# Inverse square roots of norms in a filter stage: Newton steps by column on VectorE, or Ln and Exp on ScalarE with one Newton step over all columns

## The chip, the cores and the metric

The kernel runs on one core of one Trainium2 chip. The metric is the device time of one execution in microseconds (us). The engines are named as in the profile: PE (TensorE), DVE (VectorE), ACT (ScalarE), POOL (GpSimd) and SP, each with an instruction queue of its own that is worked off in order.

## The reference

A hybrid encoder layer on x of shape (1, 1024, 1024) in float32: RMSNorm, one input projection, an S5 state-space branch, a Hyena branch with two long implicit filters, a gated merge, an output projection and a final RMSNorm. Two normalisations matter here. Each long filter is scaled by the inverse norm of its channel, and the rows of x by their inverse root mean square:

```python
def rmsnorm(x, w):
    xf = x.astype(jnp.float32)
    y = xf * lax.rsqrt(jnp.mean(xf * xf, axis=-1, keepdims=True) + RMS_EPS)
    return (y * w.astype(jnp.float32)).astype(x.dtype)

def hyena_filters(...):
    ...
    h = h * (jnp.exp(-t * jnp.abs(decay.astype(f32))) + HY_SHIFT)
    ...
    k = k * lax.rsqrt(jnp.sum(k * k, axis=0, keepdims=True) + HY_EPS)
    return jnp.fft.rfft(k, axis=0)
```

## The kernel before, in words

The kernel is one Python program that a scheduler turns into a queue of instructions for each engine. The scheduler orders by the place in the program and by readiness in its own model of time; `tc.high_priority(offset=40)` counts a block as if it were written 40 instructions earlier, and `tc.issue_after(ins)` keeps a block behind one given instruction on that engine. Buffers of a pool go round among tiles of one tag.

The first 245 us or so are the filter stage (`filters`). There are eight units, two filter orders by four quarters of 256 channels. For unit u, `filter_time` makes the filter in time in eight steps of 128 time rows: two matmuls into a PSUM tile `g` of two buffers (L333, L334), the decay by Exp on ACT (L336, tile `e`, three buffers), the product on DVE (L338), the squares on ACT (L342), sums and differences `so`, `ss`, `sd` on DVE or POOL (L349, L350), a split into a high part on ACT (L109, tile `sh`) and a low part on DVE (L113, tile `sl`), and the running sum of squares `acc` on POOL (L357, L362). `filter_freq` transforms the unit before: 48 matmuls for each of two halves of odd frequencies (L404), `even` matmuls (L414), and joins on DVE (L425 to L430). Work on the rows of x runs between the steps (`norm_in`): squares on ACT (L457), the inverse roots of eight columns (L463), scaling on ACT (L468), transposes on PE into PSUM tiles of tag `xt` (L475, two buffers), and splits (L479, L480).

`filters` steps through twelve positions i per unit, each with a piece of `filter_time` for unit u, of `filter_freq` for unit u - 1, and at every third position of `norm_in`. At i = 0 stands the norm of unit u - 1 (`filter_norm`): matmuls with a column of ones add `acc` over the partitions into tile `q` (L371, tag `xt` too), DVE adds 1e-6 (L375), `rsqrt` takes two columns (L377), and then a second part follows: two products on DVE (L381), two transposes on PE (L383) and a correction of one row of `ss` on DVE (L386), which the even matmuls with tile 0 read, at position 5. After the eighth unit both parts run with nothing of `filter_time` beside them, and the weights for the rest are then prefetched.

`rsqrt` starts from an integer estimate (L119), multiplies v by -0.5 (L121) and makes three Newton steps; each takes two instructions for every column (L125, L126), since the factor v stands as a scalar operand for each partition. A call with 2 columns has 2 + 3 x 2 x 2 = 14 instructions, the call of `norm_in` with 8 columns 50. There are eight of the one and one of the other. After the filter stage come the S5 blocks, the transforms and the projections, of which PE's queue is full.

Of the kernel before, what the change touches and what calls it, by code (L numbers as in the profile page):

```python
# [11 lines left out]
I32 = mybir.dt.int32  # L12
ALU = mybir.AluOpType
AF = mybir.ActivationFunctionType
# [86 lines left out]
class Trunk:  # L101
# [12 lines left out]

    def rsqrt(self, pool, out, v, n):

        V = self.nc.vector
        h = pool.tile([128, n], F, name="rsq_h", tag="rsq_h")
        V.tensor_scalar(out=out.bitcast(I32), in0=v.bitcast(I32), scalar1=-0.5, scalar2=float(0x5F3759DF),  # L119
                        op0=ALU.mult, op1=ALU.add)  # L120
        V.tensor_scalar(out=v, in0=v, scalar1=-0.5, scalar2=None, op0=ALU.mult)  # L121
        for _ in range(3):
            for c in range(n):
                y, z = out[:, c:c + 1], h[:, c:c + 1]
                V.scalar_tensor_tensor(out=z, in0=y, scalar=v[:, c:c + 1], in1=y, op0=ALU.mult, op1=ALU.mult)  # L125
                V.scalar_tensor_tensor(out=y, in0=z, scalar=1.5, in1=y, op0=ALU.add, op1=ALU.mult)  # L126

    def reduce_2pi(self, out, x, k):
        nc = self.nc
# [113 lines left out]
    def filters(self, ctx, top):  # L243
        tc = self.tc
# [9 lines left out]
        units = [(o, cq) for o in range(2) for cq in range(4)]  # L254
        sds = {}
        x = self.norm_in()
        for u in range(len(units) + 1):
# [16 lines left out]
            if u > 1:  # L274
                f, f0 = self.filter_freq(*units[u - 1], sds), 0
            if u == len(units):
                self.filter_norm(*units[u - 1], sds)
                c2.close()
                self.weight_pools(top)
                self.proj_pools(top)  # L280
                self.prefetch()
            for i in range(12):
                next(t, None)
                if i == 0 and u < len(units):
                    with tc.high_priority(offset=40):
                        self.filter_norm(*units[u - 1], sds)
                if i >= f0:
                    with tc.issue_after(self.f_g.ins):
                        next(f)
                if i % 3 == 0:  # L290
                    with tc.issue_after(self.f_sq.ins):
                        next(x, None)
                if i == 6 and u + 1 < len(units):
                    self.filter_load(*units[u + 1])()
# [70 lines left out]
    def filter_norm(self, o, cq, sds):  # L365
# [9 lines left out]
        nc.vector.tensor_scalar(out=qs, in0=q[:, 0:2], scalar1=1e-6, scalar2=None, op0=ALU.add)  # L375
        nrm = self.nrm[:, col:col + 2]
        self.rsqrt(up, nrm, qs, 2)  # L377
        r = q[:, NCH:]
        for ct in range(2):
            c = slice(ct, ct + 1)  # L380
# [1159 lines left out]
```

## Time and profile before

| | us |
|---|---|
| median of 3 runs | 1415.73 |
| lowest and highest | 1414.94, 1419.7 |
| the profiled execution | 1413.96 |
| its span in the trace | 1412.2 |
| busy in the span: PE, DVE, ACT, POOL | 1346.7, 1014.1, 515.1, 416.6 |
| granted TensorE clock, mean | 0.986 of full speed |

The profile is of one execution. A group row gives line, engine, operation, output and inputs with shapes and the count, then busy time in us and mean ns of one, then the idle time of the engine just before them and what ended it. In the windows, the two numbers after the stretch's name are its length and then the busy time of each engine with the number of its instructions.

### The profile page before, as it was taken

Reading aid. Unit: us, or ns where it says so; the run is one execution under the profiler, and the core shown is the slowest. Engines: PE = TensorE matmul, PEld = TensorE weight load, DVE = VectorE, ACT = ScalarE, POOL = GpSimd, SP = SyncE. Lnnn points to the kernel's source line nnn. Section 1 sums busy time; section 2 is a strip of 40 time slices with the busy share of each in tenths; the row PEclk is TensorE's granted clock in tenths of the full one; section 3 lists DMA queues with packets and bytes.
Section 4 is the critical chain, followed back from the end, with each engine's and each line's share of the span. In section 5 each row is a group of like instructions: output and inputs, shape, how many; then the busy total and the mean of one; then the engine's idle time right before and its main releaser. Section 6 shows DMA issues by size and latency. Waiting matters only on the chain.

```text
span 1412.2 us, 19536 instructions
## 1 busy us (share of the span) xinstructions
PE 1346.7 (95%) x7219; PEld 1135.9 (80%) x7219; DVE 1014.1 (72%) x1934; ACT 515.1 (36%) x737; POOL 416.6 (29%) x343
## 2 busy tenths in 40 slices
PE   5888899999999999999999997999999999999997
PEld 3777798888888887788788885998888889878886
DVE  7999997699599887414479997663899836843632
ACT  5576664222332333333322222443222234422422
POOL 3766675000000000223112213743013223322322
PEclk9999999999999999999999998999999999999999
DMA  8222224865695554566985588769888988755431
GB/s 278 94 78 75 77 100 146 200 173 137 164 301 132 124 124 103 134 173 155 307 244 173 172 241 264 216 179 315 258 268 268 292 247 245 220 161 134 139 112 64
DMA packets 188556, 257.24 MB, mean 182 GB/s; under 512 B 23069, under 2 KB 144153, under 8 KB 185724
## 3 DMA queue, kind: packets, MB, share of 16 engines
q1 hardware_dynamic: 148492, 151.32, 34.0%
q0 software_dynamic: 12608, 43.79, 15.6%
q10 hardware_dynamic: 27360, 60.88, 12.0%
q8 instruction: 57, 0.93, 0.3%
q14 instruction: 39, 0.32, 0.1%
HBM read 147.49 MB, written 76.82 MB: 159 GB/s over the span
## 4 chain that ended last, share of the span: by engine, by line
PE 72%; DVE 18%; DMA 5%; issue 3%; ACT 1%; POOL 1%; SPq 0%; ACTq 0%; DVEq 0%; POOLq 0%
PE pps L556 43%; PE ops L1441 6%; PE iv L643 5%; PE po L404 4%; PE fwo L695 3%; DMA zc<-c_zc_lo_d 2%; PE pe L414 2%; PE pps L536 2%; DVE rsq_h L125 2%; DVE e L338 1%; PE fwe L695 1%; DMA d_y<-x 1%; DVE st L1274 1%; PE zt L680 1%; DVE st L1272 1%
## 5 line engine op out<-in xcount | busy, mean ns | idle before, releaser
L512 POOL DMA_DIRECT2D wlo<-wraw x76 | 66.3, 872 | 673.3 <-ACT wlo L511 530.2
L556 PE MATMUL pps<-xh,whi 128*128 128x512 f32 x848 | 214.2, 400 | 3.2 <-DVE cv L581 3.2
L556 PE MATMUL pps<-xl,whi 128*128 128x512 f32 x848 | 212.3, 397 | 0.0
L556 PE MATMUL pps<-xh,wlo 128*128 128x512 f32 x848 | 210.2, 396 | 0.0
L556 PEld LDWEIGHTS pps<-xh,whi 128*128 128x128 f32 x848 | 158.0, 189 | 39.5 <-ACT wlo L511 3.6
L556 PEld LDWEIGHTS pps<-xh,wlo 128*128 128x128 f32 x848 | 157.9, 188 | 36.8
L556 PEld LDWEIGHTS pps<-xl,whi 128*128 128x128 f32 x848 | 157.3, 188 | 36.3 <-issue 0.2
L510 ACT CAST whi<-wraw 128x1024 fp32r<-128x1024 f32 (+1 forms) x76 | 74.7, 982 | 285.7 <-PE pps L556 254.9
L404 PE MATMUL po<-sh,fo 128*128 128x256 f32 x512 | 101.1, 292 | 6.0 <-DVE sh L111 5.1
L643 PE MATMUL iv<-ic,y 128*128 128x256 f32 (+1 forms) x752 | 97.2, 287 | 5.5 <-POOL y L113 3.1
L643 PEld LDWEIGHTS iv<-ic,y 128*128 128x128 f32 x752 | 95.4, 194 | 8.1 <-POOL y L113 4.0
L404 PEld LDWEIGHTS po<-sh,fo 128*128 128x128 f32 x512 | 84.0, 197 | 8.3 <-DVE sh L111 6.1
L357 POOL TENSOR_TENSOR acc<-acc,sq 128x512 f32<-128x512 f32 x56 | 75.9, 1356 | 24.5 <-ACT sq L342 23.0
L511 ACT ACTIVATE wlo<-whi 128x1024 fp32r<-128x1024 f32 (+1 forms) x76 | 74.9, 985 | 20.7 <-PE pps L556 20.6
L113 DVE TENSOR_TENSOR y<-yraw,y 128x512 fp32r<-128x512 f32 x60 | 55.0, 938 | 28.2 <-ACT y L109 28.2
L404 PE MATMUL po<-sl,fo 128*128 128x256 f32 x256 | 74.2, 290 | 1.0 <-DVE sl L113 1.0
L579 DVE SCALAR_TENSOR_TENSOR cv<-pps,cw,cv 128x1023 f32<-128x1023 f32 x24 | 30.7, 1281 | 59.5 <-ACT cv L578 59.5
L109 ACT CAST y<-yraw 128x512 fp32r<-128x512 f32 x64 | 39.0, 619 | 55.9 <-DMA yraw<-d_y 27.4
L404 PEld LDWEIGHTS po<-sl,fo 128*128 128x128 f32 x256 | 50.4, 197 | 2.2 <-DVE sl L113 1.3
L578 ACT ACTIVATE cv<-pps,cb,cw 128x1024 f32<-128x1024 f32 x24 | 29.0, 1208 | 62.1 <-PE pps L556 43.9
L333 PE MATMUL g<-w3h,ha 128*128 128x512 f32 x64 | 33.3, 520 | 18.6 <-DVE e L338 17.6
L695 PE MATMUL fwo<-z,zc 128*128 128x256 f32 x384 | 49.9, 283 | 0.0
(447 smaller groups left out, 2788.7 us busy)
## 6 DMA issues: line engine op xcount, KB each, us to landing
wlo<-wraw POOLq DMA_DIRECT2D x64, 512.0 KB, 5.7
wraw<-w_in SPq DMA_DIRECT2D x56, 512.0 KB, 5.2
kspec<-ko SPq DMA_DIRECT2D x32, 512.0 KB, 3.6
kt<-kspec SPq DMA_DIRECT2D x32, 512.0 KB, 5.1
yraw<-d_y SPq DMA_DIRECT2D x64, 256.0 KB, 5.3
d_y<-x ACTq DMA_DIRECT2D x28, 512.0 KB, 5.5
d_m<-cv ACTq DMA_DIRECT2D x16, 512.0 KB, 2.6
d_z<-z ACTq DMA_DIRECT2D x8, 1024.0 KB, 5.5
```

The costliest lines, as they stand in the source:

```text
L109: nc.scalar.copy(out=hi, in_=src)
L113: e.tensor_tensor(out=lo, in0=src, in1=hi, op=ALU.subtract)
L333: nc.tensor.matmul(out=ps, lhsT=ha[:, tsl], rhs=w3h, start=True, stop=False)
L357: nc.gpsimd.tensor_tensor(out=acc, in0=acc, in1=sq, op=ALU.add)
L404: nc.tensor.matmul(out=po[:, part], lhsT=fo[a][:, 12 * (jj % 2) + b], rhs=sd[4 + i][d][:, part], start=n == 0 and part == 0, stop=n == 11 ...
L510: nc.scalar.copy(out=hi, in_=raw)
L511: nc.scalar.activation(out=lo, in_=hi, func=AF.Copy, scale=-1.0)
L512: nc.gpsimd.dma_start(out=lo, in_=raw, accum_op=ALU.add)
L556: self.summed = nc.tensor.matmul(out=ps[:, hf * 512:hf * 512 + 512], lhsT=w[:, kc], rhs=part(x, kc, hf), start=a == 0 and p == 0 and kc == ...
L643: self.rotated = nc.tensor.matmul(out=dst, lhsT=lhsT, rhs=self.ic[b, j][:, cols], start=first, stop=last)
L695: nc.tensor.matmul(out=out, lhsT=zc[a][:, b], rhs=z[:, :, d, zi], start=start and n == 0, stop=stop and n == 3 * len(prods) - 1)
L1441: nc.tensor.matmul(out=pss[cs.start][:, 0:cs.stop - cs.start], lhsT=m[:, kc, ts], rhs=w[kc][:, cs], start=kc == 0 and p == 0, stop=kc == 7 ...
```

## The change

`rsqrt` takes the logarithm of all columns and then the exponential of -0.5 times it, both on ACT, in place of the integer estimate, and makes one Newton step of three DVE instructions over all columns in place of three steps by column. `filter_norm` becomes a generator with one stop, behind `rsqrt`; `filters` runs its first part at i = 0 as before and its second part at i = 3, with the same priority, ahead of that position's piece of `filter_freq`. After the last unit both parts run one after the other.

```diff
--- before.py
+++ after.py
@@ -114,16 +114,14 @@
 
     def rsqrt(self, pool, out, v, n):
 
-        V = self.nc.vector
+        nc, V = self.nc, self.nc.vector
         h = pool.tile([128, n], F, name="rsq_h", tag="rsq_h")
-        V.tensor_scalar(out=out.bitcast(I32), in0=v.bitcast(I32), scalar1=-0.5, scalar2=float(0x5F3759DF),
-                        op0=ALU.mult, op1=ALU.add)
+        nc.scalar.activation(out=h, in_=v, func=AF.Ln)
+        nc.scalar.activation(out=out, in_=h, func=AF.Exp, scale=-0.5)
         V.tensor_scalar(out=v, in0=v, scalar1=-0.5, scalar2=None, op0=ALU.mult)
-        for _ in range(3):
-            for c in range(n):
-                y, z = out[:, c:c + 1], h[:, c:c + 1]
-                V.scalar_tensor_tensor(out=z, in0=y, scalar=v[:, c:c + 1], in1=y, op0=ALU.mult, op1=ALU.mult)
-                V.scalar_tensor_tensor(out=y, in0=z, scalar=1.5, in1=y, op0=ALU.add, op1=ALU.mult)
+        V.tensor_tensor(out=h, in0=out, in1=out, op=ALU.mult)
+        V.tensor_tensor(out=h, in0=h, in1=v, op=ALU.mult)
+        V.scalar_tensor_tensor(out=out, in0=h, scalar=1.5, in1=out, op0=ALU.add, op1=ALU.mult)
 
     def reduce_2pi(self, out, x, k):
         nc = self.nc
@@ -274,7 +272,8 @@
             if u > 1:
                 f, f0 = self.filter_freq(*units[u - 1], sds), 0
             if u == len(units):
-                self.filter_norm(*units[u - 1], sds)
+                for _ in self.filter_norm(*units[u - 1], sds):
+                    pass
                 c2.close()
                 self.weight_pools(top)
                 self.proj_pools(top)
@@ -283,7 +282,11 @@
                 next(t, None)
                 if i == 0 and u < len(units):
                     with tc.high_priority(offset=40):
-                        self.filter_norm(*units[u - 1], sds)
+                        norm = self.filter_norm(*units[u - 1], sds)
+                        next(norm)
+                if i == 3 and u < len(units):
+                    with tc.high_priority(offset=40):
+                        next(norm, None)
                 if i >= f0:
                     with tc.issue_after(self.f_g.ins):
                         next(f)
@@ -375,6 +378,7 @@
         nc.vector.tensor_scalar(out=qs, in0=q[:, 0:2], scalar1=1e-6, scalar2=None, op0=ALU.add)
         nrm = self.nrm[:, col:col + 2]
         self.rsqrt(up, nrm, qs, 2)
+        yield
         r = q[:, NCH:]
         for ct in range(2):
             c = slice(ct, ct + 1)
```

## Rows read from the trace of the kernel before

**Rows 1.** The page: PE and DVE over the span, and in forty slices
```profile
PE 1346.7 (95%) x7219; PEld 1135.9 (80%) x7219; DVE 1014.1 (72%) x1934; ACT 515.1 (36%) x737; POOL 416.6 (29%) x343
...
PE   5888899999999999999999997999999999999997
...
DVE  7999997699599887414479997663899836843632
```

**Rows 2.** Busy time by engine, between the norms' starts; last row all seven
```profile
45.40:70.50 25.10, 21.47 (x119) 18.23 (x120) 24.65 (x50) 15.91 (x27) 19.30 (x19) 0.93 0.31 111
70.50:98.40 27.90, 24.40 (x149) 21.39 (x149) 26.22 (x50) 23.73 (x58) 18.90 (x20) 0.96 0.26 92
98.40:132.90 34.50, 28.81 (x168) 25.10 (x168) 33.73 (x103) 17.24 (x30) 19.79 (x21) 0.88 0.22 83
132.90:160.70 27.80, 25.77 (x160) 23.03 (x160) 27.25 (x52) 19.77 (x36) 18.48 (x20) 0.94 0.23 80
160.70:185.90 25.20, 22.20 (x144) 19.76 (x144) 24.06 (x51) 16.83 (x30) 20.78 (x20) 1.00 0.21 72
185.90:213.10 27.20, 27.14 (x184) 24.76 (x184) 27.10 (x55) 19.09 (x32) 20.45 (x23) 1.00 0.25 96
213.10:237.50 24.40, 23.01 (x152) 20.59 (x151) 22.87 (x47) 10.71 (x19) 17.50 (x18) 1.00 0.22 87
45.40:237.50 192.10, 172.80 (x1066) 152.87 (x1067) 185.87 (x398) 123.29 (x225) 135.20 (x139) 0.96 0.24 88
```

**Rows 3.** Who waited for whom, 45 to 245 us: total, times, longest
```profile
ACT sq L342 <- DVE e L338: 19.1, 12, 5.5
...
PE g L333 <- DVE e L338: 12.8, 9, 3.1
...
PEld pe L414 <- DVE ss L386: 2.5, 3, 1.1
```

**Rows 4.** The chain that ended last, 45 to 245 us, by line
```profile
by line: PE po L404 19.8%; PE pe L414 12.6%; DVE rsq_h L125 12.1%; DVE e L338 9.3%; issue 5.7%; DVE sl L113 5.0%; DVE nrm L126 3.7%; DVE ko L429 2.6%; DVE xl L480 2.6%; PE g L333 2.5%; DVE ko L430 2.4%; PE g L334 2.1%; DVE so L350 2.1%; DVE
```

**Rows 5.** Groups of DVE instructions by line, 0 to 260 us
```profile
L125 DVE SCALAR_TENSOR_TENSOR rsq_h<-nrm,qs 128x1 f32<-128x1 f32 x48 | 21.9, 490 | 0.2
...
L126 DVE SCALAR_TENSOR_TENSOR nrm<-rsq_h,nrm 128x1 f32<-128x1 f32 x48 | 10.2, 233 | 0.0
L125 DVE SCALAR_TENSOR_TENSOR rsq_h<-rs,ssq 128x1 f32<-128x1 f32 x24 | 8.2, 358 | 0.0
...
L126 DVE SCALAR_TENSOR_TENSOR rs<-rsq_h,rs 128x1 f32<-128x1 f32 x24 | 4.4, 196 | 0.0
...
L119 DVE TENSOR_SCALAR nrm<-qs 128x2 int32<-128x2 int32 x8 | 3.1, 384 | 0.1
```

**Rows 6.** Instructions in order of time, DVE then POOL, from 46 us
```profile
46.05 1.42 DVE L125 SCALAR_TENSOR_TENSOR rsq_h<-nrm,qs 128x1 f32<-128x1 f32 x2
47.39 0.27 DVE L126 SCALAR_TENSOR_TENSOR nrm<-rsq_h,nrm 128x1 f32<-128x1 f32 x2
...
46.18 2.62 POOL L357 TENSOR_TENSOR acc<-acc,sq 128x512 f32<-128x512 f32 x2 [0.39 <-ACT acc L342]
```

**Rows 7.** Group of small ACT instructions, one column each
```profile
L1458 ACT ACTIVATE rs<-ssq 128x1 f32<-128x1 f32 x8 | 2.4, 296 | 0.2
```

**Rows 8.** ACT's instructions in order of time around a table load
```profile
15.65 0.41 ACT L217 ACTIVATE h<-u 64x256 f32<-64x256 f32 x1
16.08 1.28 ACT L336 ACT_TABLE_LOAD   x1
17.38 1.95 ACT L336 ACTIVATE e<-dec,negt 128x512 f32<-128x512 f32 x3
```

**Rows 9.** A group of table loads on ACT, of the later stages
```profile
L747 ACT ACT_TABLE_LOAD x5 | 6.4, 1283 | 0.1
```

**Rows 10.** DVE in order of time, the norm of the sixth unit
```profile
185.90 0.15 DVE L375 TENSOR_SCALAR qs<-q 128x2 f32<-128x2 f32 x1
...
197.70 0.35 DVE L386 SCALAR_TENSOR_TENSOR ss<-q,ss 1x256 f32<-1x256 f32 x1
```

## The prediction

> **What bounds the kernel now.** The page comes first: over the whole span PE is busy 95% and DVE 72%, but in the second to sixth of its forty slices (about 35 us each) DVE stands at nine tenths or more, PE at eight to nine [rows 1]. That is the filter stage, and all nine calls of `rsqrt` lie in it. I then cut the stage within 0.7 us of the eight starts of L375, the first DVE instruction of each norm, which gives seven units of 24.4 to 34.5 us [rows 2]. The reader is to see two engines near their limit: over the 192.10 us DVE is busy 185.87, PE 172.80, ACT 123.29. PE is idle 192.10 - 172.80 = 19.3 us, and the waits name the cause: 12.8 us of it is the first filter matmul (L333) waiting for DVE's `e` (L338) to free its PSUM bank; PE's weight loads wait 2.5 us for L386 [rows 3]. So DVE sets the pace, yet PE is close behind. The chain of the same stretch agrees: 12.1% of 200 us, 24 us, stands on L125, and 3.7%, 7 us, on the first form of L126 [rows 4].
>
> One unit stands out. The third is 34.5 us long because the 8-column call for the rows of x falls in it as well, 8.2 + 4.4 = 12.6 us of records [rows 5].
>
> **What is removed.** A call with 2 columns has 14 DVE instructions, one with 8 columns 50; eight and one of them make 162. By line, L125 costs 21.9 + 8.2, L126 10.2 + 4.4 and L119 3.1 us [rows 5]. Nine instructions (L121, the factor -0.5) stay, so 153 go with some 48 us of records. Neighbouring records on DVE overlap by about 0.08 us (46.05 + 1.42 = 47.47, but the next starts at 47.39) [rows 6], so the time on the engine is nearer 48 - 153 x 0.08 = 36 us. Why so much for single columns? The pair of L125 that starts at 46.05 lasts 1.42 us, while POOL runs L357 from 46.18, and the like pair of L126 behind it 0.27 [rows 6]. An instruction that reads two SBUF operands seems to be held until POOL's ends.
>
> **What is added on DVE.** Three instructions with two SBUF operands per call, 27 in all; the means of L126 and L125 (0.233 and 0.490 us) bound them, 6 to 13 us. I take 9, since the three lie in a row and only the first often meets POOL's instruction. Net, DVE gives back 36 - 9 = 27 us. Part of the holds may move to the next instruction of this kind (L113, L349); that price is between nothing and some 10 us, and I take 4, leaving 23.
>
> **What is added on ACT.** Eighteen small activations: a single column with a bias takes 0.296 us today [rows 7], so at most 0.6 us per call; I take 0.5, as no bias is read. Then the function tables. A load takes 1.283 us, and nothing else lies around it: the activation ahead ends at 16.06, the load starts at 16.08 and the next activation at 17.38 [rows 8]. Where functions alternate later, a line loads again and again: five times at L747 [rows 9]. The filter stage uses Exp throughout, at L336. If Ln comes with a table that lacks Exp, each call loads twice: 18 x 1.283 = 23.1 us. If one table holds both, one load may do for all. No row shows which; I take 18, as those repeated loads are the nearest row. ACT has 192.10 - 123.29 = 68.8 us idle in the units, so most of it is hidden beside DVE and PE. The cover is thin in the second unit: ACT is busy 23.73 of 27.90 there, 4.17 us free, and a call takes 2 x 1.283 + 0.5 = 3.1 of them. What stays on the path is `e` (L336) coming late for L338 and squares (`sq`) coming late for POOL; between nothing and the whole 3.1 us per call, I take 0.25 us, because `e` has three buffers and the present waits of ACT are mostly for DVE itself (19.1 us) [rows 3].
>
> The Trainium skill, ScalarE: Activation LUTs, section What ACT_TABLE_LOAD costs, puts a switch at about 2.66 us, of which 1.38 are a drain. This speaks against the change: by it the loads would take an estimated 18 x 2.66 = 48 us of ACT, the second unit would gain nothing, and the sum below would be 11.5 us instead of 12.6. The rows show no such drain beside the 1.283 us [rows 8], so the sum goes by the rows.
>
> **What is moved.** The second part of a norm, two L381, two transposes L383 and one L386, is issued three steps later; in the last call both parts still run together. A step is about a twelfth of a unit, 2.1 us. No DMA belongs to it, and it passes nothing on SP's or POOL's queue; on DVE it lets the `e`, `so` and `sl` instructions of steps 1 to 3 go ahead, on PE their matmuls. Today L386 starts 12 us after L375 in the sixth unit (197.70 against 185.90) [rows 10], later than three steps, and its user is the even transform of step 5. I cost the move at nothing. Its cover is those steps: if it is gone, PE waits at L414 as it does now for L386, and the x transposes wait for the PSUM bank that `q` holds; today's waits behind L386 sum to 2.5 us over the stage [rows 3], and that bounds it. The wait that it adds in place of the DVE chain is ACT's: Ln stands at the head of ACT's queue until L375 is done, with `e`, `sq` and `sh` behind it. PE has to wait for none of these at once.
>
> **The sum.** DVE could give back 23 us, but no unit can shrink by more than PE's idle time in it unless PE gets quicker. Unit by unit that idle time is 3.6, 3.5, 5.7, 2.0, 3.0, 0.1 and 1.4 us [rows 2]. DVE's removed records of the eight 2-column calls average (21.9 + 10.2 + 3.1) / 8 = 4.4 us, so PE is the tighter limit in nearly all; ACT cuts the second to about 4.17 - 3.1 = 1.1. Sum: 3.6 + 1.1 + 5.7 + 2.0 + 3.0 + 0.1 + 1.4 = 16.9 us. Less 9 x 0.25 = 2.3 for late `e`, and less about 2 for units where DVE and PE still miss each other: **12.6 us**. The last norm, after 237.5, meets matmuls of the eighth unit and the first projections on PE; I cost its longer latency on ACT at nothing, and without that cover at the 3.1 us above. After the stage PE is full, so a stage that ends earlier should move everything behind it.
>
> The profiled execution took 1413.96 us (span 1412.2 and 1.8 around it), 1.8 below the median 1415.73. 1413.96 - 12.6 = 1401.4; I forecast **1401 us**, with 1394 to 1408 as this case's own range. What I can't price from both sides is PE's clock: the first four units had 0.88 to 0.96 of the full 2.4 GHz (the lower level being 1.2), with PE idle most in the unit with 0.88. If fewer gaps bring 1.00, the 172.80 busy us could shrink by up to 4%, 6.9 us more; if not, nothing.
>
> **Rivals.** First, **no change that can be told** (1412, chance 0.16): the holds by POOL move to L113 and L349 instead of vanishing, and PE, which is nearly full in the sixth unit (27.14 of 27.20), becomes the bound everywhere. Then only the third unit gains, some 5.7 us, late `e` takes back 2.3 and the moved holds some 1.5: 1413.96 - 1.9. Against it: the 12.8 us of PE's waits for `e` stand on DVE's queue, and 144 - 27 = 117 fewer two-operand instructions meet POOL.
>
> Second, **slower** (1422, chance 0.09): the Ln of each call blocks ACT in order. It waits for L375, which sits in a DVE queue that is busy 97%; then two loads; and all that time no `e`, `sq` or `sh` is made, so DVE and POOL run dry and PE after them. From 16.9 / 8 = 2.1 us per call on the path the gain is undone. If the 3.1 us of ACT's own work are bare in eight calls, it is 8 x 3.1 - 16.9 = 7.9 us above 1413.96. Against it: ACT is idle a third of the stage, and today ACT is the one that waits for DVE, 19.1 us [rows 3].
>
> Third, **one table for both functions** (1398, chance 0.07): 17 of 18 loads are missing, 21.8 us of ACT; the second unit gains its whole 3.5 instead of 1.1, and about 1 us less is lost to late `e`: 1401.4 - 2.4 - 1.0. The Trainium skill, ScalarE: Activation LUTs, section Table sets: the hidden batching unit, says just this: Ln followed by Exp needs one load, because one set has both. No row here bears on it.
>
> **The numbers.** The forecast has 0.68. About 0.3% (4.2 us) is what a measurement of this kernel can tell from no change. Faster by more: 0.68 + 0.07 = 0.75; within: 0.16; slower: 0.09. The range takes the forecast's own spread, the third rival, half of the clock's possible gift at the low end, and the second case up to 1414 at the high end; the slower case is left out: 1391 to 1414.
>
> **What would show it.** Right: the third unit falls from 34.5 to about 28 us, the L333 waits for `e` fall well below 12.8 us, L125 and L126 shrink to 27 short records, 18 loads appear on ACT at the two new lines, and the PE idle time of the stage falls by about 13 us. The stage after L375's last start keeps its length. Wrong would be: waits of DVE for ACT's `e` or of ACT's Ln for DVE of more than 1 us per call; the same total of DVE records with L113 and L349 longer; or a stage shorter by 13 us and an end that is not.

## The result and the profile after

The changed kernel takes **1423.97 us** (median; 1422.1 to 1426.1) against 1415.81 us of the kernel before, run on the same chip: ratio **1.0053, 95% interval 1.0034 to 1.0071**. It is slower by about 8 us where 1401 us were forecast. The profiled execution took 1426.1 us, its span 1424.3. It is the slowest of its five, and the profiled one of the kernel before, 1413.96 us, lies below all five of that kernel, so the two profiles are 12.1 us apart and not 8. By line, L378 is now the first instruction of a norm (L375 before), L119 the Ln, L120 the exponential, L121 the scaling by -1/2, L122 to L124 the Newton step, L339 ACT's `e`, L341 DVE's `e`.

The page of the changed kernel, the lines that answer [rows 1]:

```profile
PE 1352.6 (95%) x7219; PEld 1142.6 (80%) x7219; DVE 987.0 (69%) x1808; ACT 540.9 (38%) x773; POOL 410.5 (29%) x343
...
PE   5789898999999999999999997999999999999997
...
DVE  7877887589699887514469997653899835833632
```

DVE has 27 us less to do over the span, and in the second to sixth slices it no longer stands at nine tenths. PE has not moved into the room. Busy time between the norms' starts of the changed kernel, to be laid beside [rows 2] (length; busy time of PE, PEld, DVE, ACT, POOL; granted clock; DMA share; GB/s):

```profile
46.40:75.70 29.30, 22.12 (x116) 18.79 (x117) 24.48 (x39) 19.17 (x33) 18.04 (x19) 0.88 0.25 93
75.70:102.60 26.90, 23.02 (x132) 19.54 (x131) 21.10 (x37) 25.30 (x57) 19.44 (x20) 0.94 0.19 66
102.60:135.00 32.40, 29.66 (x196) 27.58 (x195) 24.83 (x50) 25.36 (x43) 19.25 (x20) 0.95 0.27 102
135.00:164.10 29.10, 25.35 (x165) 22.20 (x164) 24.53 (x43) 21.98 (x37) 19.70 (x21) 1.00 0.26 98
164.10:188.90 24.80, 21.75 (x138) 19.13 (x138) 21.07 (x40) 19.67 (x33) 19.80 (x20) 1.00 0.16 62
188.90:215.70 26.80, 25.88 (x180) 23.75 (x179) 22.33 (x42) 19.08 (x32) 18.95 (x20) 1.00 0.30 118
215.70:246.30 30.60, 26.41 (x158) 23.32 (x158) 22.48 (x38) 17.71 (x28) 19.56 (x20) 0.94 0.14 54
46.40:246.30 199.90, 174.18 (x1071) 154.30 (x1072) 160.82 (x282) 148.29 (x259) 134.73 (x138) 0.96 0.23 85
```

The stage is 199.9 us long instead of 192.1. DVE's busy time fell by 185.87 - 160.82 = 25.0 us, but its time without work rose from 192.10 - 185.87 = 6.2 to 199.90 - 160.82 = **39.1 us**. PE's idle time rose from 19.3 to 25.7. From the last norm's start to the end of the span are 1424.3 - 246.3 = 1178.0 us (before 1412.2 - 237.5 = 1174.7). Of the 12.1 us between the two profiles 7.8 lie in the seven units, 1.0 ahead of them and 3.3 behind.

What DVE and PE wait for is in the waits of the changed kernel, 46 to 247 us (total, times, longest; its first row answers one of [rows 3]):

```profile
PE g L336 <- DVE e L341: 12.4, 9, 3.1
...
DVE sl L113 <- ACT sh L109: 10.0, 7, 2.3
DVE qs L121 <- ACT rsq_h L119: 9.5, 5, 3.9
...
PE q L387 <- DVE qs L385: 6.9, 7, 2.0
...
DVE ko L433 <- PE po L408: 5.7, 5, 2.2
...
DVE rsq_h L122 <- ACT nrm L120: 4.7, 4, 1.9
...
ACT rsq_h L119 <- DVE qs L378: 4.4, 1, 4.4
...
DVE e L341 <- ACT e L339: 3.8, 3, 1.5
...
PE pe L418 <- DVE ke L430: 3.4, 4, 1.5
```

The like rows of the kernel before, 45 to 238 us:

```profile
DVE sl L113 <- ACT sh L109: 2.1, 3, 1.0
...
PE q L383 <- DVE qs L381: 2.0, 3, 0.9
...
PE pe L414 <- DVE ke L426: 1.5, 3, 0.6
```

PE's wait for DVE's `e`, the first row, is as large as it was (12.8). DVE waits for ACT: 10.0 us for `sh` (2.1 before), 9.5 us at L121 for the Ln, 4.7 us at L122 for the exponential, 3.8 for `e`. The Ln itself waited for DVE once only, 4.4 us. What PE waits longer for is the norm itself: 6.9 us at the two transposes (L387), whose products need the inverse root, against 2.0; and 3.4 us at the even transform, for `ke`, against 1.5.

The groups of table loads and of the new small functions on ACT, 0 to 270 us (busy us, mean ns, idle before), against [rows 7, 9]:

```profile
L119 ACT ACT_TABLE_LOAD x9 | 11.5, 1283 | 0.2
...
L339 ACT ACT_TABLE_LOAD x6 | 7.7, 1283 | 0.1
L120 ACT ACT_TABLE_LOAD x4 | 5.1, 1283 | 0.1
...
L119 ACT ACTIVATE rsq_h<-qs 128x2 f32<-128x2 f32 x8 | 1.6, 204 | 4.5 <-DVE qs L378 4.4
L120 ACT ACTIVATE nrm<-rsq_h 128x2 f32<-128x2 f32 x8 | 1.5, 193 | 0.0
```

Nineteen loads where before had one, at L336 [rows 8]: 18 x 1.283 = 23.1 us. One call seen from both engines, ACT first, then DVE, in order of time (start, duration, in brackets the idle time ahead and who ended it), against [rows 6, 8]:

```profile
78.20 1.28 ACT L119 ACT_TABLE_LOAD   x1
79.50 0.20 ACT L119 ACTIVATE rsq_h<-qs 128x2 f32<-128x2 f32 x1
79.61 0.60 ACT L109 CAST sh<-so 128x512 fp32r<-128x512 f32 x1
80.23 1.28 ACT L339 ACT_TABLE_LOAD   x1
81.53 0.72 ACT L339 ACTIVATE e<-dec,negt 128x512 f32<-128x512 f32 x1
...
82.77 0.19 ACT L120 ACTIVATE nrm<-rsq_h 128x2 f32<-128x2 f32 x1
```

```profile
75.72 0.15 DVE L378 TENSOR_SCALAR qs<-q 128x2 f32<-128x2 f32 x1
79.73 0.17 DVE L121 TENSOR_SCALAR qs<-qs 128x2 f32<-128x2 f32 x1 [3.86 <-ACT rsq_h L119]
79.81 0.68 DVE L341 SCALAR_TENSOR_TENSOR e<-e,g 128x512 f32<-128x512 f32 x1
80.41 0.68 DVE L113 TENSOR_TENSOR sl<-so,sh 128x512 fp32r<-128x512 f32 x1
82.99 0.16 DVE L122 TENSOR_TENSOR rsq_h<-nrm 128x2 f32<-128x2 f32 x1 [1.89 <-ACT nrm L120]
```

L378 is done at 75.87. The Ln stands behind other work of ACT and behind its own load, and ends at 79.70. L121 scales in place what the Ln reads, so it must wait, and in DVE's queue `e` and `sl` stand behind it: 3.86 us in which DVE does nothing. Not all of it is lost by the order on DVE. The `e` behind L121 also needs the filter matmuls that end at 78.76,

```profile
78.36 0.40 PE L337 MATMUL g<-w3l,ha 128*128 128x512 f32 x1
```

so it was held for about 1.0 us; and `sl` needs `sh`, which ACT itself made only behind the load and the Ln (80.21). Then the load for `e` (80.23) comes between the two functions, and L122 waits 1.89 us more.

### The profile page after: what moved, and what is told of

Read it like the earlier page. It is cut to its first block, busy times and chain, and to the rows that moved or that the text cites. A ratio compares the mean times of both kernels' runs of the same rounds, so it can differ in the third digit from the quotient of the medians.

```text
span 1424.3 us, 19442 instructions
## 1 busy us (share of the span) xinstructions
PE 1352.6 (95%) x7219; PEld 1142.6 (80%) x7219; DVE 987.0 (69%) x1808; ACT 540.9 (38%) x773; POOL 410.5 (29%) x343
## 3 DMA queue, kind: packets, MB, share of 16 engines
q10 hardware_dynamic: 27360, 60.88, 11.9%
## 4 chain that ended last, share of the span: by engine, by line
PE 72%; DVE 11%; DMA 4%; ACT 3%; issue 2%; SPq 0%; POOL 0%; DVEq 0%; ACTq 0%; POOLq 0%
PE pps L560 45%; PE ops L1445 6%; PE iv L647 5%; PE fwo L699 3%; DMA zc<-c_zc_lo_d 2%; PE po L408 2%; PE pps L540 2%; PE fwe L699 2%; PE pe L418 1%; PE zt L684 1%; DVE st L1278 1%; DVE st L1276 1%; DVE e L341 1%; PE s5ps L1228 1%; PE s5ps L1255 1%
## 5 line engine op out<-in xcount | busy, mean ns | idle before, releaser
L647 PEld LDWEIGHTS iv<-ic,y 128*128 128x128 f32 x752 | 99.4, 202 | 4.4 <-DVE y L113 2.1
L647 PE MATMUL iv<-ic,y 128*128 128x256 f32 (+1 forms) x752 | 100.7, 295 | 2.4 <-DVE y L113 1.8
L360 POOL TENSOR_TENSOR acc<-acc,sq 128x512 f32<-128x512 f32 x56 | 79.3, 1416 | 38.9 <-ACT sq L345 29.2
L113 DVE TENSOR_TENSOR y<-yraw,y 128x512 fp32r<-128x512 f32 x60 | 54.3, 926 | 30.2 <-ACT y L109 30.2
L336 PE MATMUL g<-w3h,ha 128*128 128x512 f32 x64 | 33.5, 523 | 18.2 <-DVE e L341 17.3
```

Source lines behind the costliest of these rows:

```text
L113: e.tensor_tensor(out=lo, in0=src, in1=hi, op=ALU.subtract)
L336: nc.tensor.matmul(out=ps, lhsT=ha[:, tsl], rhs=w3h, start=True, stop=False)
L360: nc.gpsimd.tensor_tensor(out=acc, in0=acc, in1=sq, op=ALU.add)
L647: self.rotated = nc.tensor.matmul(out=dst, lhsT=lhsT, rhs=self.ic[b, j][:, cols], start=first, stop=last)
```

## The experiments

All are stated as a ratio to the kernel before, run in the same series, with the 95% interval. For the profiled execution of each I give the seven units' length from the first to the eighth norm's start, DVE's busy time in it, and the rest, DVE's **gaps**. These three are of one execution each, and the program behind the eighth norm's start took between 1174.4 and 1185.4 us in them, so units and ratio need not agree to the last us. In the edits, a line of three dots stands for lines left out.

```
kernel                                   ratio [95%]               units   DVE busy   gaps
before                                   1                         192.1   185.9       6.2
changed                                  1.0053 [1.0034, 1.0071]   199.9   160.8      39.1
 1 one table, queues planned anew        1.0007 [0.9996, 1.0018]   189.0   165.6      23.4
 2 changed, without the move             1.0058 [1.0046, 1.0071]   200.0   162.3      37.7
 3 before, with the move                 1.0011 [0.9998, 1.0023]   193.6   188.1       5.5
 4 changed, scaled into its own tile     1.0046 [1.0033, 1.0058]   199.4   160.1      39.3
 5 three steps over all columns, on DVE  1.0052 [1.0033, 1.0071]   201.3   181.5      19.8
 6 the same with the move                1.0060 [1.0042, 1.0077]   201.4   182.8      18.6
 7 one step on DVE, nothing on ACT       0.9934 [0.9910, 0.9959]   182.7   166.3      16.4
 8 one table at the changed order        0.9988 [0.9978, 0.9998]   191.0   169.7      21.3
 9 18 loads at the order of run 1        1.0090 [1.0074, 1.0105]   200.4   161.4      39.0
10 no wait for ACT, changed order        1.0012 [1.0000, 1.0024]   189.9   169.4      20.5
11 run 7 with DVE's time put back        1.0044 [1.0029, 1.0059]   196.6   181.2      15.4
12 run 8 with DVE's time put back        1.0116 [1.0094, 1.0137]   210.4   185.1      25.3
13 before with more DVE time             1.0180 [1.0162, 1.0197]   211.1   202.2       8.9
14 before, priority 20 in place of 40    0.9999 [0.9985, 1.0012]   192.0   185.7       6.3
15 before, priority 60 in place of 40    1.0008 [0.9995, 1.0021]   192.8   186.8       6.0
16 before with two buffers for so        1.0045 [1.0031, 1.0058]   200.5   188.6      11.9
17 run 1 with two buffers for so         0.9915 [0.9898, 0.9931]   183.7   165.5      18.2
18 run 7 with two buffers for so         0.9902 [0.9886, 0.9917]   176.6   167.3       9.3
```

### One part at a time

**Run 1**, the loads: one table that holds both functions is put ahead of the first exponential.

```diff
         x = self.norm_in()
+        with tc.issue_after(self.f_sin.ins):
+            self.nc.scalar.preload_act_table_set("natural_log_exp_and_others")
```

> The changed kernel, but the one function table that has both Ln and Exp is loaded ahead of the filter stage's first Exp, so that the 19 loads of the stage become 1. Theory A (the 24 us of table loads make ACT late, and DVE, which works in order, waits for sh, Ln and Exp): 1402 to 1408 us, DVE idle in the units back from 39 to under 20 us. Rival B (DVE waits because the scaling of v by -0.5, written in place, stands right behind L378 and must wait until Ln has read v; a load more or less matters little): 1418 to 1423. Rival C (the second part of the norm comes too late, the move): 1420 to 1425.

All 18 loads are gone, and the time is 1417.24 us, 1.0007 of before: the loads matter, but taking them away only brings the kernel back to before. This fits neither theory whole, and it opens the second question: where did the relief of DVE go?

**Run 2**, the move undone (both parts of the norm at step 0):

```diff
-                        norm = self.filter_norm(*units[u - 1], sds)
-                        next(norm)
-                if i == 3 and u < len(units):
-                    with tc.high_priority(offset=40):
-                        next(norm, None)
+                        for _ in self.filter_norm(*units[u - 1], sds):
+                            pass
```

> The changed kernel with both parts of the norm at position 0, as before; the new rsqrt alone. Theory A: nothing told apart from the changed kernel, 1420 to 1428 us. Rival B: the same. Rival C (the move costs): 1408 to 1416, as before or better.

**Run 3**, the move alone, in the kernel before (the same lines the other way, with the `yield` behind `rsqrt`):

> The kernel before with the second part of the norm three steps later, the old rsqrt. Theory A and rival B: 1412 to 1418 us, as before. Rival C: 1420 us or more.

With and without: 1425.01 and 1423.97; in before: 1.0011, an interval that holds 1. The move costs and brings nothing that can be told.

**Run 4**, the scaling by -1/2 into a tile of its own, issued ahead of the Ln, so that it waits for nobody:

```diff
+        w = pool.tile([128, n], F, name="rsq_w", tag="rsq_w")
+        V.tensor_scalar(out=w, in0=v, scalar1=-0.5, scalar2=None, op0=ALU.mult)
         nc.scalar.activation(out=h, in_=v, func=AF.Ln)
         nc.scalar.activation(out=out, in_=h, func=AF.Exp, scale=-0.5)
-        V.tensor_scalar(out=v, in0=v, scalar1=-0.5, scalar2=None, op0=ALU.mult)
...
```

> The changed kernel with the product -0.5 v in a tile of its own, ahead of Ln, so that this DVE instruction waits for nothing on ACT; tables and move as in the changed kernel. Theory A: the wait goes over to the next DVE instruction that needs Exp, 1418 to 1424 us. Rival B: 1405 to 1413. Rival C: 1420 to 1425.

1422.51 us, 1.0046 against 1.0053: the intervals overlap, so no gain can be told, as theory A said. The wait at L121, 9.5 us in the profile, is only where DVE stood; without it DVE stands at the next instruction that needs ACT (8.3 us in the units at the reader of the exponential; the gaps are 39.3 us, in the changed kernel 39.1).

### The loads at an order held fixed

Each edit lets the planner write every engine's queue anew, so a pair of runs differs in more than its edit. In runs 8 and 9 the loads alone are put in or left out **after** the queues are written: `put_loads` sets a load into ACT's queue right ahead of each instruction that it is told.

**Run 8**: the changed kernel's own queues, one load ahead of the first exponential.

```diff
         Trunk(tc, ins, outs).run()
+    first = []
+    put_loads(nc, "natural_log_exp_and_others", lambda i: not first and is_func(i, AF.Exp) and not first.append(i))
...
```

> The changed kernel with each engine's queue in the very order that it has there, but with the one table for Ln and Exp loaded once ahead of the first Exp, put in after the order was made; 18 loads are gone and nothing else differs. Theory A (the loads cost what was lost): 1408 to 1416 us. Rival F (the new order of the queues costs it, whatever the loads): 1420 to 1425.

**Run 9**: run 1's queues, with a load ahead of each Ln; the loads back for the exponentials follow from it (9, 5 and 4 loads at three lines, 18 together).

```diff
         Trunk(tc, ins, outs).run()
+    put_loads(nc, "natural_log", lambda i: is_func(i, AF.Ln))
...
```

> The other way round: the queues in the order of the one-table run (1417 us), and 18 loads put in ahead of Ln and of the Exp behind it, nothing else. Theory A: 1424 to 1432 us. Rival F: 1416 to 1420.

The kernels of a pair were measured in different series, so the ratios are compared. At the changed kernel's order the loads cost 1.0053 - 0.9988 = 0.0065 of before's time, **9.2 us**, at run 1's order 1.0090 - 1.0007 = 0.0083, **11.8 us**; within each pair the intervals don't touch, and the units say the same (8.9 and 11.4 us). Of 23.1 us of loads, 0.40 and 0.51 came out at the end, 1.0 and 1.3 us per call. That settles the loss against before. Run 8 also shows that without loads the gain is 0.0012 of the time, though DVE has 16.2 us less to do.

### Is DVE's time what the end waits for?

**Run 7**: no ScalarE function; the integer estimate of before and one Newton step over all columns. (Two of before's three steps are left out.)

```diff
-        nc.scalar.activation(out=h, in_=v, func=AF.Ln)
-        nc.scalar.activation(out=out, in_=h, func=AF.Exp, scale=-0.5)
+        V.tensor_scalar(out=out.bitcast(I32), in0=v.bitcast(I32), scalar1=-0.5, scalar2=float(0x5F3759DF),
+                        op0=ALU.mult, op1=ALU.add)
```

> The changed kernel with Ln and Exp replaced by the old integer estimate on DVE, so one Newton step over all columns and no ACT at all; two Newton steps are left out, so the norms are coarse. DVE has 5 instructions per call against 14 or 50. This is the most that relief of DVE can give with no price on ACT. Theory D: 1398 to 1406 us. Rival E: 1411 to 1418, with DVE idle in the units of 20 us or more and PE idle still near 19.

It gains 0.0066, between the two forecasts. (Its profiled execution, 1405.04 us, is the fastest of six; the median is 1408.85.) Either DVE's time counts after all, or run 7 met a good order of the queues. Runs 11, 12 and 13 keep the queues of run 7, run 8 and before in the stage and add 117 small DVE instructions in all, which nobody reads, behind the inverse square roots:

```diff
+        made = [nc.vector.scalar_tensor_tensor(out=s[:, k:k + 1], in0=s[:, 126:127], scalar=s[:, 127:128],
+                                               in1=s[:, 126:127], op0=ALU.mult, op1=ALU.mult).ins.name
+                for k in range(n0, n0 + count(n))]
...
+    put_dummies(nc, spare, RECORDED, lambda n: 9 if n == 2 else 45)
```

> Every engine's queue as in the kernel with one Newton step and no ScalarE function (which took 182.65 us for the seven units and 0.9934 of before), with 117 small VectorE instructions of 128x1 added right behind the last instruction of each inverse square root, 9 in each unit and 45 in the call on eight columns; nobody reads what they write. Theory D (that kernel's gain is VectorE time): at the 0.14 to 0.31 us that such instructions took in before they add 16 to 36 us to VectorE, the units go back to 190 us or more and the time to 1.000 of before or above. Rival F (its gain is its order of the queues): VectorE's 16 us of idle time takes them in; units within 2 us of 182.65, the time 0.992 to 0.996 of before.

> The changed kernel at its own order of the queues without the 18 loads (units 191.07 us, 0.9988 of before), with the 117 small VectorE instructions added behind the last one of each inverse square root, 9 in each unit and 45 in the call on eight columns; nobody reads what they write. At the order of the kernel with no ScalarE function they took 14.9 us of VectorE and lengthened the units by 13.9, at the order of before 16.4 and 19.0. Theory S (VectorE's 21 us of idle time at this order are gaps that its own queue runs through one after another, so its time counts in full here too): 0.008 to 0.013 above, so 1.007 to 1.012 of before. Rival (at this order another strand sets the end and the idle time is slack): 0.998 to 1.003.

> Every engine's queue as in the kernel before, with the same 117 small VectorE instructions added behind the last one of each inverse square root; nobody reads what they write. The prediction's premise (VectorE sets the pace of the units, with 6.2 us idle of 192.1): the 16 to 36 us of added work come out at the end but for those 6 us, so 1.007 to 1.021 of before. Rival (VectorE's work is only one strand among several, and a unit's slack takes it in): below 1.004.

The sums over the units of run 7 and of runs 11, 12 and 13 (columns as in the table of units above):

```profile
45.40:228.10 182.70, 167.87 (x1075) 149.76 (x1076) 166.31 (x290) 124.70 (x226) 135.25 (x139) 0.99 0.26 94
```

```profile
45.50:242.10 196.60, 170.73 (x1075) 152.08 (x1076) 181.24 (x398) 125.12 (x226) 134.40 (x139) 0.97 0.24 88
```

```profile
45.30:255.70 210.40, 178.75 (x1071) 158.69 (x1072) 185.11 (x389) 126.44 (x242) 133.22 (x139) 0.92 0.22 81
```

```profile
45.10:256.20 211.10, 181.10 (x1065) 156.96 (x1066) 202.24 (x505) 123.64 (x225) 133.88 (x139) 0.91 0.21 81
```

Run 11: DVE +14.9 us, units +13.9. Run 12 against run 8: +15.5 and +19.4. Run 13 against before: +16.4 and +19.0. At every order the added time comes out in full, even where DVE stands idle 21 us of the stage. That the stage is as long as DVE's work and gaps together is so by definition; what the runs show is that the gaps don't take the added work in. So they are no slack for it: DVE's queue runs through work and waits one after the other. But the added work stands at one place of each norm, ahead of the products that PE's transposes wait for, and PE's wait there grew from 3.7 to 15.5 us (run 7 to 11), from 3.5 to 18.3 (run 8 to 12) and from 2.0 to 9.2 (before to 13). Whether DVE's time counts in full elsewhere in its queue wasn't tried. (The parts above 1:1 go with a granted clock of 0.92 and 0.91 instead of 0.96, and PE's busy time is 6.7 and 8.3 us longer.)

The ratios of runs 10 to 13 say more than the stage. In these four, two DMA transfers of constants (`icp`, `ic`), which matmuls far behind the stage read, are issued later in POOL's queue than in the kernels that they are compared with, and PE stands waiting for the first of them, in run 13 for 20.2 us:

```profile
PE iv L642 <- DMA icp<-c_ic_d: 20.2, 1, 20.2
```

It is 18.7, 13.7 and 13.5 us in runs 10, 11 and 12; in before and in runs 7 and 8 all waits of these matmuls (tile `iv`) together are 11.2 to 12.4 us. Behind the eighth norm's start the program is 3.5, 1.2, 2.8 and 10.7 us longer in runs 10, 11, 12 and 13 than in run 8, run 7, run 8 and before. For these runs the units are the figure to read.

### What makes the gaps: ACT's two functions, or the order?

**Run 10** keeps run 8's queues in the stage and takes away what makes DVE wait: the Ln and the exponential keep their places but work on a spare tile, and DVE makes the integer estimate in place of the scaling. `swap` puts the new instruction at the old one's place, with the wait that is given.

```diff
+        swap(old[ln], nc.scalar.activation(out=c, in_=s[:, 0:n], func=AF.Ln), [])
+        swap(old[ex], nc.scalar.activation(out=d, in_=c, func=AF.Exp, scale=-0.5), None)
+        swap(old[scale], nc.vector.tensor_scalar(out=out.bitcast(I32), in0=v.bitcast(I32), scalar1=-0.5, scalar2=float(0x5F3759DF),
+                                                 op0=ALU.mult, op1=ALU.add), [read[0], read[0].wait_value])
+        swap(old[sq], nc.vector.tensor_tensor(out=h, in0=out, in1=out, op=ALU.mult), [read[0], seen[scale][1]])
+        swap(old[mul], nc.vector.scalar_tensor_tensor(out=h, in0=h, scalar=-0.5, in1=v, op0=ALU.mult, op1=ALU.mult), None)
...
```

> The changed kernel at its own order of every queue and without the 18 loads (that run: units 191.07 us, 0.9988 of before), and now VectorE no longer waits for ScalarE's Ln and Exp: the two still stand at their places in ScalarE's queue but read and write a spare tile, and the first of the four VectorE instructions of each inverse square root makes the integer estimate in place of the scaling by -1/2, which is folded into the third. (The factor -1/2 that the norm's later work expects in v is left out, and where VectorE read ScalarE's exponential e under the cover of the wait that went, a wait for that e alone stands.) Theory H (what the change loses beyond the loads is VectorE standing in its queue for ScalarE's two functions, which come behind other work of ScalarE): units 181 to 186 us, 0.990 to 0.996, as in the kernel with no ScalarE function. Rival F (the order of the queues loses it): units 189 us or more, 0.997 to 1.001.

Units 189.9, 1.1 us less than in run 8: DVE's waits for ACT's two functions, once the loads are gone, are not what loses the relief, and theory H falls. (The ratio, 1.0012, has the 3.5 us behind the stage in it.) Run 10 and run 7 do the same work on DVE, and yet run 10's units are 7.2 us longer, 3.1 of it records and 4.1 gaps. The order is not all that differs: ACT's two functions still stand in run 10's queue. What DVE waits for, 46 to 240 us in run 10, then 46 to 230 us in run 7:

```profile
DVE ko L434 <- PE po L409: 7.3, 5, 3.2
DVE sl L113 <- ACT sh L109: 6.7, 6, 2.3
DVE ss L391 <- PE q L388: 3.1, 2, 2.7
```

```profile
DVE sl L113 <- ACT sh L109: 6.3, 6, 1.8
DVE ke L429 <- ACT eo L425: 5.3, 2, 4.8
...
DVE ko L433 <- PE po L408: 0.6, 1, 0.6
```

The wait for `sh` is about the same. The joins of even and odd transforms differ: 7.3 us at `ko` against 0.6, while run 7 has 5.3 at `ke`, 4.8 of it one wait for ACT's `eo` in the first unit. In all the joins wait 8.3 us (with 1.0 at `ke`, not shown) and 5.9. The difference is plain in the seventh unit (30.2 us in run 8, 24.6 in run 7, 4.4 of the 5.6 us being gaps). There the joins stand in a row at the end of DVE's queue. DVE in order of time in run 8:

```profile
229.58 0.68 DVE L430 TENSOR_TENSOR ke<-pe,eo 128x512 f32<-128x512 f32 x1
233.49 0.69 DVE L433 TENSOR_TENSOR ko<-ke,po 128x512 f32<-128x512 f32 x1 [3.23 <-PE po L408]
234.10 0.68 DVE L434 TENSOR_TENSOR ko<-ke,po 128x512 f32<-128x512 f32 x1
236.34 0.69 DVE L433 TENSOR_TENSOR ko<-ke,po 128x512 f32<-128x512 f32 x1 [1.57 <-PE po L408]
```

4.8 us of waits for PE's odd transform, with nothing else between them in DVE's queue. In run 7 two instructions of `e` stand between the joins, and the same unit has 0.6 us of that wait.

**Runs 5 and 6**: the three Newton steps of before over all columns, on DVE, at step 0 and with the move.

```diff
-            for c in range(n):
-                y, z = out[:, c:c + 1], h[:, c:c + 1]
-                V.scalar_tensor_tensor(out=z, in0=y, scalar=v[:, c:c + 1], in1=y, op0=ALU.mult, op1=ALU.mult)
-                V.scalar_tensor_tensor(out=y, in0=z, scalar=1.5, in1=y, op0=ALU.add, op1=ALU.mult)
+            V.tensor_tensor(out=h, in0=out, in1=out, op=ALU.mult)
+            V.tensor_tensor(out=h, in0=h, in1=v, op=ALU.mult)
+            V.scalar_tensor_tensor(out=out, in0=h, scalar=1.5, in1=out, op0=ALU.add, op1=ALU.mult)
```

> The kernel before with its three Newton steps over all columns instead of by column: 11 DVE instructions per call instead of 14 or 50, nothing on ACT, no move. Theory D (what DVE gives back is worth its time on the path as long as ACT is not asked): some 63 instructions fewer, 39 of them in the third unit; 1406 to 1411 us. Rival E (the stage is tied by the order of waits among DVE, ACT, POOL and PE, and relief of DVE only makes DVE idle): 1413 to 1418.

> Three Newton steps over all columns on VectorE, as in the run that came out at 1.0052 of before, and with the norm's second part three steps later. The move alone cost nothing in two other pairs of kernels. Theory C (the three steps over all columns cost this of themselves): 1.004 to 1.007 again. Rival F (that run met a bad order of the queues, and another order of the same work gives another time): more than 0.003 away from 1.0052.

In run 5 both theories miss. The two runs have 4.4 and 3.1 us less of DVE's time and are 0.005 to 0.006 slower; the gaps are 13.6 and 12.4 us larger, at `sl`, `ko` and `ke` again (7.1, 6.1 and 3.0 us in run 5). Run 6 came out as its theory C said, yet its largest waits are nearly those of run 5 (`sl` 7.3 us, `ke` 3.3), so it was no second order, and it doesn't tell C from F. That the order makes these gaps is argued from where they stand; it wasn't tried at before's order.

**Runs 14 and 15**: before with another priority for the norm, meant as two more orders.

```diff
-                    with tc.high_priority(offset=40):
+                    with tc.high_priority(offset=20):
```

> The kernel before with the norm counted as 20 instructions earlier instead of 40: the same instructions, another order. If order by itself moves the time (rival F), some 5 us or more away from 1416 on either side; if not, 1413 to 1419.

> The kernel before with the norm counted as 60 instructions earlier instead of 40: as the run with 20. Rival F: 5 us or more away from 1416 on either side; else 1413 to 1419.

The queues hardly differ from before's, so these runs show only how little before's time moves, 0.0009 between them; they don't bear on the order.

### A version that beats both

Runs 16 to 18 give the tile `so`, through which DVE, POOL and ACT pass the sums of `e`, a second buffer, in before, run 1 and run 7:

```diff
-so = wp.tile([128, 2, NCH], F, name="so", bufs=1)
+so = wp.tile([128, 2, NCH], F, name="so", bufs=2)
```

> The control of the run with two so buffers: the kernel before with so in two buffers, nothing else. If DVE is the bound there, 1413 to 1418 us, nothing to tell; if the so loop ties the kernel before too, 1405 to 1411.

> The changed kernel with the one table and the tile so (sums and differences of the odd rows) in two buffers instead of one. If the loop of so on POOL, sh on ACT and sl on DVE through the single so buffer is what ties the stage (rival E's mechanism): 1403 to 1411 us, waits of POOL for sl well under 16 us. If not: 1415 to 1419, as with one buffer.

> The kernel with one Newton step and no ScalarE function (0.9934 of before) and a second buffer for the tile so. With the one-table kernel the second buffer took 0.0092 off, on before it added 0.0045. If a second buffer pays wherever VectorE has idle time: 0.984 to 0.989 of before, the fastest of all. If the two gains are the same slack of PE taken up twice: 0.991 to 0.995.

In before it loses (1.0045, outside both of its forecasts; its gaps go from 6.2 to 11.9 us), in run 1 it gains 0.0092 (1406.80 us, as forecast), in run 7 some 0.003 more (between its two forecasts; the two intervals overlap a little): **1402.65 us, 0.9902**, the fastest of all, with gaps of 9.3 us, the least of the kernels with one Newton step. Like run 7 it leaves out two Newton steps of before. The changed kernel's own idea is kept in run 17: Ln and exponential on ACT with one table, 0.9915.

## Why the prediction was wrong

**The step that failed first** is the term for what of ACT's loads "stays on the path", 0.25 us per call, 2.3 us in all. It measured 9.2 us at the changed kernel's order and 11.8 at another: 1.0 to 1.3 us per call. The argument was that ACT has 68.8 us without work, so that loads lie beside DVE and PE. But the wait doesn't come from ACT's total. DVE takes its queue in order, and L121, L122, `e` and `sl` all need a result of ACT that now comes one or two loads later. Of the two late results that the prediction named, `e` made 3.8 us of DVE's waits; the two functions made 9.5 + 4.7 = 14.2 and `sh` 10.0. PE was to wait "for none of these at once", with 2.5 us behind L386 as the bound; its wait at the transposes just ahead of that line went from 2.0 to 6.9 us. The text's bounds (nothing to 3.1 us per call) held; the value in them was taken too low.

**The step that failed next** is the sum itself: DVE's relief as a gain in each unit, up to PE's idle time in it, 16.9 us. PE's idle time never went down as that needs: it is 25.7 us in the changed kernel, and 191.0 - 172.0 = 19.0 in run 8, without loads, against 19.3 before. PE's waits in run 8, 46 to 238 us, show where the relief went:

```profile
PE g L336 <- DVE e L341: 7.9, 8, 1.7
...
PE pe L418 <- DVE ke L430: 6.0, 4, 2.8
...
PE q L387 <- DVE qs L385: 3.5, 4, 2.1
```

The wait for `e` fell by 12.8 - 7.9 = 4.9 us, as the forecast had it, and came back at the even transform (6.0 against 1.5) and the transposes (3.5 against 2.0). The premise that DVE sets the pace held for the time added in runs 11 to 13, and the clock gave nothing back (0.96 again). What was missing is that DVE's queue has gaps beside its work, and that an edit which lets the queues be planned anew can make more of them; the kernel before had only 6.2 us. Run 8 has 16.2 us less work and 15.1 us more gaps: a gain of 1.1. Every new order met in these runs that gave DVE less work had 9 to 23 us of gaps without the loads, 38 to 39 with them. The unit-by-unit minimum allowed for some of this with "about 2" us. That the order of the queues makes these gaps is argued, as said above, not shown.

**The moved holds**, costed at 4 us between nothing and some 10, were low without the loads. The group of `sl` in the units, before and then in run 8:

```profile
L113 DVE TENSOR_TENSOR sl<-so,sh 128x512 fp32r<-128x512 f32 x27 | 20.8, 769 | 2.2 <-ACT sh L109 2.1
```

```profile
L113 DVE TENSOR_TENSOR sl<-so,sh 128x512 fp32r<-128x512 f32 x27 | 26.4, 978 | 6.7 <-ACT sh L109 6.7
```

That is 26.4 - 20.8 = 5.6 us, and the products (L381, then L385) went from 369 to 733 ns, 9.7 - 4.7 = 5.0 us more. The three new instructions took 12.0 us there where 9 were forecast. So DVE gave back 16.2 us instead of 23. In the changed kernel the two groups grew by 1.8 and 2.1 us only and the new instructions took 8.1, which is why its 25.0 us look like the forecast. A likely reason is that a DVE that stands waiting meets fewer of POOL's instructions (`sl` 837 ns); no run tests it.

**What was right.** Eighteen loads of 1.283 us; ACT 25.0 us busier; ACT's two functions 0.20 + 0.19 us per call against 0.5. The move at nothing (runs 2 and 3). No drain shows beside a load: L119's ends at 79.48 and the Ln starts at 79.50. The Trainium skill (ScalarE: Activation LUTs, What ACT_TABLE_LOAD costs) gives 2.66 us a switch, of which 1.283 are the load; this trace agrees on the load and shows none of the rest.

**What the runs leave unanswered.** The last norm's longer latency was put at nothing, or at 3.1 us without cover. The program behind it was 3.3 us longer in the changed kernel's profile, but as much as 2.9 us longer in run 1, without loads, so this can't be put down to it.

**The signs of being wrong** that the prediction named hardly came: DVE's waits for `e` and the Ln's for DVE are 3.8 and 4.4 us over nine calls, under 1 us per call. The wait that came, of DVE for the Ln and the exponential, was not among them. Of the signs of being right the loads and the short records came; the third unit went to 32.4 us instead of about 28, and PE's wait for `e` stayed at 12.4.

**The rivals.** The slower one had the right sign and the right engine, and its threshold of 2.1 us per call was counted from a gain that wasn't there. That its 1422 us lie near the 1424 measured is luck: it sets 24.8 us of ACT's work against a gain of 16.9 us, where the runs have some 9 against 1. Its place was only half right: it had the Ln waiting for DVE and ACT's queue behind it; the trace has that once (4.4 us), and DVE's queue standing behind the Ln five times (9.5 us). The first rival, no change, comes nearest to run 8, without the loads (0.9988): holds did move to L113 (5.6 us), as it says, but PE was not full (19.0 us idle). The third rival fell: the two functions were not served by one table until it was put there by hand, and then the time was 1417 and not 1398. The Trainium skill (ScalarE: Activation LUTs, Table sets: the hidden batching unit) says that Ln followed by Exp needs one load, since one set has both. That set exists (run 1 has no load behind the one put there), but by itself this program switched at every call, 18 loads.

**What stays open.** Where run 7's order is better than run 8's is shown for the seventh unit (5.6 us) only. That before's order is unusually free of gaps is seen in the runs at hand, not explained. Run 5 was not tried at before's order.

## What to carry to other kernels

Moving work from a busy engine to an idle one puts a handshake into the busy engine's queue: count what stands behind the waiting instruction there, not the idle time of the engine that takes the work, and look for a table switch in every alternation of functions. Where a planner writes the queues, read the busy engine's gaps beside its busy time, and judge an edit at an order held fixed as well as planned anew; here two plans for nearly the same work on DVE (runs 7 and 10) differed by 7.2 us in the stage, about as much as the changed kernel lost there (7.8). To learn whether an engine's time counts, add idle work to it at a fixed order, at more than one place of its queue, and look whether anything far from the place has moved as well.

## What the runs showed of the hardware that was not expected

- Ln and exponential in turn load a table 18 times in nine calls, at 1.283 us each; with the set that holds both loaded by hand there is none, and both functions take 0.19 to 0.21 us on 128x2 and 128x8.
- The same small DVE instruction lasts 0.16 us or over 1.2: L123 took 166 ns on 128x8 in the changed kernel and 1221 ns in run 8. The 117 added instructions of 128x1, all columns their own, added 14.9 to 16.4 us to DVE's busy time in the units, 0.14 to 0.15 us each (108 of them lie there).
- PE's granted clock in the stage was 0.96 of full in before, 0.91 in run 13 with longer gaps on PE (30.0 us against 19.3) and 0.99 in run 7 with shorter ones (14.8); PE's busy time was 181.1 and 167.9 us for nearly the same matmuls (1065 and 1075 records).
